# Top-2 gate dispatch on one core: transfers beside a change of direction are issued in smaller pieces

## The chip, the core and the metric

The kernel runs on one core of one Trainium2 chip. The metric is the device time of one execution in microseconds; where several runs are given, their median counts. The kernel before takes 242.45 us in the median of 9 runs (242.27 to 242.94).

## What is computed

For each of 16 x 1024 = 16384 tokens there are 8 router logits and a row of 512 fp32 values. The two largest softmax probabilities are scaled to sum to one, and the row is written out twice, once times each of the two weights.

```python
def reference(x, router_logits, k):          # x [16,1024,512], router_logits [16,1024,8], k = 2
    logits_max = np.max(router_logits, axis=-1, keepdims=True)
    probs = np.exp(router_logits - logits_max)
    probs = probs / np.sum(probs, axis=-1, keepdims=True)
    topk_indices = np.argsort(probs, axis=-1)[..., -k:]
    topk_probs = np.take_along_axis(probs, topk_indices, axis=-1)
    topk_probs = topk_probs / np.sum(topk_probs, axis=-1, keepdims=True)
    x_expanded = x[:, :, np.newaxis, :].repeat(k, axis=2)
    return (x_expanded * topk_probs[..., np.newaxis]).astype(np.float32)
```

In bytes: x is 33.55 MB, the logits are 0.52 MB, the output is 67.11 MB. Everything that is read is read once, and everything that is written is written once.

## The kernel before

The 16384 tokens are laid over 128 partitions, 128 tokens ("rows" below) on each, so that the rows of one partition lie one behind the other in memory. A row is 2 KB of input and 4 KB of output. A transfer of n rows therefore moves, for each partition, one unbroken stretch of n x 2 KB (a load) or n x 4 KB (a store).

First the logits come in with one transfer (L72). `top2_weights` finds the largest and second largest logit by a tree of max and min on VectorE, and ScalarE makes the two weights from their difference with two sigmoids (L41, L42). The weights of all rows stay in `WA`.

The rows are then worked through in two groups of 64 (`GROUP`). For each group:

- Four loads of 16 rows each (4.19 MB) go into `xs`, a buffer of 64 rows (L93 and L94).
- Six multiplications on VectorE (L97) follow `plan`: rows 0 to 15 into `osp`; rows 16 to 31 in place over `xs` rows 0 to 31; rows 32 to 39 and 40 to 47 into the two halves of `osp`; rows 48 to 55 and 56 to 63 over the two halves of `xs` rows 32 to 63. An output row is twice as long as an input row, which is why 16 rows fill 32 rows of `xs`.
- After each multiplication one store writes its rows (L103): 16, 16, 8, 8, 8, 8 rows, which is 8.39 MB for 16 rows and 4.19 MB for 8.

All transfers are issued by SyncE (SP) in the order of the program, and all go through its one queue. SP issues in order: an issue that has to wait holds up those behind it. What the issues wait for comes from the buffers: a store waits for its multiplication; the multiplication of rows 32 to 39 waits for the store that reads `osp`; the loads of the second group wait for the stores that still read their part of `xs`. The framework places these waits from the regions that each operation reads and writes.

Below, "load 1" to "load 4" and "store 1" to "store 6" are the transfers of a group in program order. Between the last load of a group and its first store, and between the last store of the first group and the first load of the second, the queue changes direction: load to store, store to load, load to store, three times in all.

Of the kernel before, what the change touches and what calls it, by code (L numbers as in the profile page):

```python
# [1 line left out]

# [4 lines left out]

F32 = mybir.dt.float32
ALU = mybir.AluOpType
ACTF = mybir.ActivationFunctionType  # L10
P = 128


def top2_weights(nc, pool, logits, M, E):

    hi, lo, n = None, None, E
    while n > 1:  # L20
        n //= 2
        if hi is None:
            a, b = logits[:, :, 0:n], logits[:, :, n : 2 * n]
            nhi = pool.tile([P, M, n], F32, tag=f"hi{n}")
            nlo = pool.tile([P, M, n], F32, tag=f"lo{n}")
            nc.vector.tensor_tensor(nhi, a, b, op=ALU.max)  # L26
            nc.vector.tensor_tensor(nlo, a, b, op=ALU.min)  # L27
        else:
            a, b = hi[:, :, 0:n], hi[:, :, n : 2 * n]
            nhi = pool.tile([P, M, n], F32, tag=f"hi{n}")  # L30
            nlo = pool.tile([P, M, n], F32, tag=f"lo{n}")
            tmp = pool.tile([P, M, n], F32, tag=f"tmp{n}")
            nc.vector.tensor_tensor(tmp, lo[:, :, 0:n], lo[:, :, n : 2 * n], op=ALU.max)  # L33
            nc.vector.tensor_tensor(nlo, a, b, op=ALU.min)  # L34
            nc.vector.tensor_tensor(nlo, nlo, tmp, op=ALU.max)  # L35
            nc.vector.tensor_tensor(nhi, a, b, op=ALU.max)  # L36
        hi, lo = nhi, nlo
    dlt = pool.tile([P, M], F32, tag="dlt")
    nc.vector.tensor_tensor(dlt, hi[:, :, 0], lo[:, :, 0], op=ALU.subtract)  # L39
    WA = pool.tile([P, M, 2], F32, tag="WA")  # L40
    nc.scalar.activation(WA[:, :, 0], dlt, ACTF.Sigmoid, scale=-1.0)  # L41
    nc.scalar.activation(WA[:, :, 1], dlt, ACTF.Sigmoid, scale=1.0)  # L42
    return WA


@with_exitstack
def kernel(
    ctx: ExitStack,
    tc: tile.TileContext,
    x: bass.AP,  # L50
    router_logits: bass.AP,
    k: bass.AP,
    out: bass.AP,
):
    nc = tc.nc
    B, S, D = x.shape
    E = router_logits.shape[-1]
    N = B * S
    assert int(k) == 2 and E == 8 and N % P == 0
    M = N // P  # L60

    GROUP = 64
    L = 16
    x_v = x.rearrange("b s d -> (b s) d").rearrange("(p m) d -> p m d", p=P)
    o_v = out.rearrange("b s k d -> (b s) k d").rearrange("(p m) k d -> p m k d", p=P)
    rl_v = router_logits.rearrange("b s e -> (b s) e").rearrange(
        "(p m) e -> p m e", p=P
    )

    wpool = ctx.enter_context(tc.tile_pool(name="wpool", bufs=1))  # L70
    logits = wpool.tile([P, M, E], F32)
    nc.sync.dma_start(logits, rl_v)  # L72
    WA = top2_weights(nc, wpool, logits, M, E)

    xs = wpool.tile([P, GROUP, D], F32)
    osp = wpool.tile([P, L, 2, D], F32)


    low = xs[:, : 2 * L, :].rearrange("p (r k) d -> p r k d", k=2)
    high = xs[:, 2 * L :, :].rearrange("p (r k) d -> p r k d", k=2)  # L80
    h = L // 2
    plan = [
        (0, L, osp),
        (L, L, low),
        (2 * L, h, osp[:, :h]),
        (2 * L + h, h, osp[:, h:]),
        (3 * L, h, high[:, :h]),
        (3 * L + h, h, high[:, h:]),
    ]

    for g in range(M // GROUP):
        m0 = g * GROUP
        for r in range(0, GROUP, L):  # L93
            nc.sync.dma_start(xs[:, r : r + L, :], x_v[:, m0 + r : m0 + r + L, :])  # L94
        for r, n, og in plan:
            rows = slice(m0 + r, m0 + r + n)
            nc.vector.tensor_tensor(  # L97
                og,
                xs[:, r : r + n, :].unsqueeze(2).to_broadcast([P, n, 2, D]),
                WA[:, rows, :].unsqueeze(3).to_broadcast([P, n, 2, D]),  # L100
                op=ALU.mult,
            )
            nc.sync.dma_start(o_v[:, rows], og)  # L103


# [1 line left out]
_INS = ['x', 'router_logits', 'k']  # L107
_OUTS = [((16, 1024, 2, 512), 'float32')]

_NUMBERS = {'k': 2}  # L110


# [26 lines left out]
```

## Time and profile before

| | |
|---|---|
| median of 9 runs | 242.45 us |
| the profiled execution's own time | 242.83 us |
| its span in the profile | 241.0 us |
| VectorE busy | 142.0 us (59% of the span) |
| ScalarE busy | 1.8 us |
| DMA packets' time, as a share of 16 engines' span | 98.4% |
| bytes moved, mean rate over the span | 101.19 MB, 420 GB/s |
| loads on L94 | 8, 4096 KB each |
| stores on L103 | 12: 8 of 4096 KB, 4 of 8192 KB |
| multiplication of 16 rows (128x16384) | 17.2 us |
| multiplication of 8 rows (128x8192) | 8.7 us |

The span is what the hardware profiler sees of one execution; 1.83 us of the execution's own time lie around it. A core has 16 DMA engines, and each transfer is cut into packets that are spread over them. The DMA share is the time in which these engines had a packet in hand. Times inside the profile count from the start of the span. The trace also keeps a record of each packet, with its start, its duration and its size.

### The profile page before, as it was taken

The numbers are of one execution on the slowest core, as the hardware profiler recorded it, in microseconds if no ns is written. First come the engines' busy times: TensorE is split into PE (matmuls) and PEld (weight loads), VectorE is DVE, ScalarE is ACT, GpSimd is POOL, SyncE is SP. The second block draws the span as 40 slices with busy tenths as digits, with TensorE's granted clock in tenths as the row PEclk, the third lists the DMA queues.
The fourth block names the chain that finished last, engine by engine and source line by source line (L and its number), as shares of the span: only waits on it lengthen the run. The fifth ranks groups of instructions, "written<-read, shape, count | busy, mean of one in ns | idle before, by whom it ended". The sixth has DMA issues, their size and how long they took to land.

```text
span 241.0 us, 112 instructions
## 1 busy us (share of the span) xinstructions
DVE 142.0 (59%) x23; ACT 1.8 (1%) x3; POOL 0.2 (0%) x4
## 2 busy tenths in 40 slices
DVE  2369999900399999400000999997007999990000
ACT  2000000000000000000000000000000000000000
POOL 0000000000000000000000000000000000000000
DMA  7999999998989899999999999999999999999994
GB/s 272 435 435 435 430 430 397 386 522 348 522 348 522 348 435 435 435 435 435 430 381 430 435 435 430 430 424 468 402 468 402 468 402 402 435 430 435 435 435 212
DMA packets 3024, 101.19 MB, mean 420 GB/s; under 512 B 336, under 2 KB 336, under 8 KB 464
## 3 DMA queue, kind: packets, MB, share of 16 engines
q1 hardware_dynamic: 3024, 101.19, 98.4%
HBM read 34.08 MB, written 67.11 MB: 420 GB/s over the span
## 4 chain that ended last, share of the span: by engine, by line
DMA 46%; DVE 36%; issue 7%; SPq 0%; DVEq 0%
DMA out_dram<-osp 27%; DVE osp L97 22%; DMA xs<-in_x_dram 19%; DVE xs L97 14%; SPq L72 0%; SPq L103 0%; DVEq L97 0%
## 5 line engine op out<-in xcount | busy, mean ns | idle before, releaser
L97 DVE TENSOR_TENSOR osp<-xs,WA 128x8192 f32<-128x8192 f32 (+1 forms) x6 | 69.0, 11534 | 70.2 <-DMA xs<-in_x_dram 40.0
L97 DVE TENSOR_TENSOR xs<-xs,WA 128x8192 f32<-128x8192 f32 (+1 forms) x6 | 69.2, 11536 | 0.2
L26 DVE TENSOR_TENSOR nhi<-logits 128x512 f32<-128x512 f32 x1 | 0.7, 692 | 4.4 <-DMA logits<-in_router_logits_dram 4.4
L41 ACT ACT_TABLE_LOAD x1 | 1.3, 1283 | 0.7 <-PEq L120 0.7
L33 DVE TENSOR_TENSOR tmp<-nlo 128x256 f32<-128x256 f32 (+1 forms) x2 | 0.7, 354 | 0.0
L36 DVE TENSOR_TENSOR nhi<-nhi 128x256 f32<-128x256 f32 (+1 forms) x2 | 0.7, 352 | 0.0
L35 DVE TENSOR_TENSOR nlo<-nlo,tmp 128x256 f32<-128x256 f32 (+1 forms) x2 | 0.7, 352 | 0.0
L34 DVE TENSOR_TENSOR nlo<-nhi 128x256 f32<-128x256 f32 (+1 forms) x2 | 0.7, 352 | 0.0
L27 DVE TENSOR_TENSOR nlo<-logits 128x512 f32<-128x512 f32 x1 | 0.7, 686 | 0.0
L41 ACT ACTIVATE WA<-dlt 128x128 f32<-128x128 f32 x1 | 0.3, 314 | 6.2 <-DVE dlt L39 6.2
L39 DVE TENSOR_TENSOR dlt<-nhi,nlo 128x128 f32<-128x128 f32 x1 | 0.3, 292 | 0.0
L42 ACT ACTIVATE WA<-dlt 128x128 f32<-128x128 f32 x1 | 0.3, 298 | 0.0
L120 POOL MEMSET const-bfloat16-1.0<- 128x1 bf16 x1 | 0.1, 103 | 0.0
L120 POOL MEMSET const-uint8-127<- 128x1 uint8 x1 | 0.1, 102 | 0.0
L120 POOL MEMSET const-float32-1.0<- 128x1 f32 x1 | 0.1, 100 | 0.0
L120 POOL MEMSET const-float32-0.0<- 128x1 f32 x1 | 0.1, 98 | 0.2 <-issue 0.2
## 6 DMA issues: line engine op xcount, KB each, us to landing
xs<-in_x_dram SPq DMA_DIRECT2D x8, 4096.0 KB, 36.6
out_dram<-osp SPq DMA_DIRECT2D x4, 4096.0 KB, 20.7
out_dram<-xs SPq DMA_DIRECT2D x4, 4096.0 KB, 22.7
logits<-in_router_logits_dram SPq DMA_DIRECT2D x1, 512.0 KB, 3.7
out_dram<-osp SPq DMA_DIRECT2D x2, 32.2
out_dram<-xs SPq DMA_DIRECT2D x2, 34.3
```

The costliest lines, as they stand in the source:

```text
L26: nc.vector.tensor_tensor(nhi, a, b, op=ALU.max)
L27: nc.vector.tensor_tensor(nlo, a, b, op=ALU.min)
L33: nc.vector.tensor_tensor(tmp, lo[:, :, 0:n], lo[:, :, n : 2 * n], op=ALU.max)
L34: nc.vector.tensor_tensor(nlo, a, b, op=ALU.min)
L35: nc.vector.tensor_tensor(nlo, nlo, tmp, op=ALU.max)
L36: nc.vector.tensor_tensor(nhi, a, b, op=ALU.max)
L39: nc.vector.tensor_tensor(dlt, hi[:, :, 0], lo[:, :, 0], op=ALU.subtract)
L41: nc.scalar.activation(WA[:, :, 0], dlt, ACTF.Sigmoid, scale=-1.0)
L42: nc.scalar.activation(WA[:, :, 1], dlt, ACTF.Sigmoid, scale=1.0)
L97: nc.vector.tensor_tensor(og, xs[:, r : r + n, :].unsqueeze(2).to_broadcast([P, n, 2, D]), WA[:, rows, :].unsqueeze(3).to_broadcast([P, n, ...
L120: nc = _bacc.Bacc("TRN2", target_bir_lowering=False, num_devices=1)
```

## The change

The loads of a group are cut into eight transfers of 4, 4, 8, 16, 16, 8, 4 and 4 rows, in place of four of 16. The first store of a group (16 rows) is issued as four transfers of 4 rows, and the last (8 rows) as two of 4 rows. The four stores between stay whole, and so do all six multiplications. The order of work on SP is otherwise the same.

```diff
+LOADS = [4, 4, 8, 16, 16, 8, 4, 4]
+STORE_ROWS = {0: 4, 56: 4}
...
     for g in range(M // GROUP):
         m0 = g * GROUP
-        for r in range(0, GROUP, L):
-            nc.sync.dma_start(xs[:, r : r + L, :], x_v[:, m0 + r : m0 + r + L, :])
+        r = 0
+        for n in LOADS:
+            nc.sync.dma_start(xs[:, r : r + n, :], x_v[:, m0 + r : m0 + r + n, :])
+            r += n
         for r, n, og in plan:
             rows = slice(m0 + r, m0 + r + n)
             nc.vector.tensor_tensor(
...
-            nc.sync.dma_start(o_v[:, rows], og)
+            for i in range(0, n, STORE_ROWS.get(r, n)):
+                t = STORE_ROWS.get(r, n)
+                nc.sync.dma_start(
+                    o_v[:, rows.start + i : rows.start + i + t], og[:, i : i + t]
+                )
```

In numbers: 21 transfers become 37 (1 for the logits, 16 loads, 20 stores). Beside a change of direction stand now loads of 4 rows (1.05 MB, 8 KB for a partition) and stores of 4 rows (2.10 MB, 16 KB for a partition), where loads of 16 rows (32 KB) and stores of 16 rows (64 KB) or 8 rows (32 KB) stood.

## The prediction

> **What bounds the kernel now.** I read the page first, for the engines and the DMA.
>
> ```profile
> DMA  7999999998989899999999999999999999999994
> GB/s 272 435 435 435 430 430 397 386 522 348 522 348 522 348 435 435 435 435 435 430 381 430 435 435 430 430 424 468 402 468 402 468 402 402 435 430 435 435 435 212
> q1 hardware_dynamic: 3024, 101.19, 98.4%
> ```
>
> The one queue keeps the 16 DMA engines busy for 98.4% of the span, and only the first and the last slice show real idle time. VectorE is busy 59%. So the time is that of the transfers, and the question is at what rate they run. (A packet's bytes count where it starts, so 522 and 348 in turn are one even rate seen through slices.) That the queue never runs dry is seen in the chain of waits and in SP's own waits:
>
> ```profile
> 1.16 12.96 DMA xs<-in_x_dram
> 31.48 32.56 DMA out_dram<-osp
> 99.28 33.51 DMA xs<-in_x_dram
> 150.13 31.88 DMA out_dram<-osp
> 208.16 8.69 DVE xs L97
> ```
> ```profile
> SPq L94 <- DMA out_dram<-xs: 21.6, 2, 11.5
> ```
>
> Columns of the first: start, duration, what. Store 1 of group 1 is issued at 31.48 and lands at 64.04, though 8.39 MB need only some 19 us: it stands behind loads 2 to 4. Load 1 of group 2, issued at 99.28, lands at 132.79 behind the stores. The last multiplication ends at 216.85, and the last store, issued at 216.88, lands 23.2 us later by the list of issues, at 240.08. In the second view SP waits 21.6 us for stores to leave `xs` before loads 3 and 4 of group 2 (issued at 112.40 and 122.89); when the later of them goes out, three loads (29 us of work) are still queued. No transfer starts late.
>
> These landings split the span into stretches that can be priced. From 182.01 to 240.08 there are only stores: store 2 (8.39 MB) and stores 3 to 6 (4.19 MB each), 25.17 MB in 58.07 us, 433.4 GB/s. That is the plain rate. The other stretches each hold one change of direction:
>
> - 14.12 to 64.04, loads 2 to 4 and store 1, 20.97 MB: 49.92 us, 48.39 at the plain rate, so 1.53 lost.
> - 64.04 to 132.79, stores 2 to 6 and load 1, 29.36 MB: 68.75 us against 67.75, so 1.00 lost.
> - 132.79 to 182.01, as the first: 49.22 us, so 0.83 lost.
>
> Together 3.36 us. The windows around the changes show where:
>
> ```profile
> 39.60:43.70 4.10, 4.10 (x1) 0.00 (x0) 0.00 (x0) 1.00 1.11 352
> 119.40:124.90 5.50, 0.00 (x0) 0.00 (x0) 0.00 (x0) 1.00 1.01 375
> 157.90:162.70 4.80, 4.80 (x1) 0.00 (x0) 0.00 (x0) 1.00 1.08 423
> 30.00:39.60 9.60, 9.57 (x2) 0.00 (x0) 0.00 (x0) 1.00 1.01 437
> ```
>
> The last two numbers of a row are DMA share and GB/s. The engines stay busy (share about 1) while the rate falls to 352 and 375 GB/s: packets take longer, nobody waits. The packet records say which. A 32 KB packet takes 1.21 us everywhere, but the last two of load 4 on each engine take 1.2 to 2.3 us in group 1 (up to 2.0 in group 2); at the store-to-load change the last store packet and the first two or three load packets take 1.3 to 1.9. By the mean over the engines this is 1.31, 0.76 and 0.51 us, 2.58 in all; the other 0.8 of the 3.36 is that the engines drift apart, from 0.6 to 1.8 us between first and last, and the last counts.
>
> **The change part by part.**
>
> *Sixteen more transfers on the DMA engines.* Each adds 8 packets and one completion per engine. The packet records price this: 4.19 MB in 32 KB packets stand 9.681 us apart from completion to completion on an engine, 8.39 MB in 64 KB packets 19.319. 2 x 9.681 - 19.319 = 0.043 us is the price of eight more packets and one more completion. 16 x 0.043 = +0.69 us, on the path, since the queue is never empty. From packet durations instead (queue lines of two windows: 1.214 us for 32 KB, 2.417 for 64 KB, so 0.011 for a packet, 0.09 for eight) it would be 16 x 0.09 = 1.4. I take 0.69, since durations overlap and completions don't, and keep 1.4 as the upper end. No packet of 8 or 16 KB is in the trace; the logits' 4 KB packets take 0.156 to 0.159 us once running, 26 GB/s on an engine where 32 KB packets make 27, so the middle sizes hold no surprise.
>
> *A rule that speaks against this.* In the stretch after 182.01 five stores run back to back at 433.4 GB/s, so a transfer's own latency does not show when the next one is queued. The Trainium skill ("DMA: Bandwidth & Descriptors", Rules for kernel authors, and Anatomy of one DMA) advises to merge small transfers, with 1 MiB as the size to reach, which the 4-row loads just do, and fits some 2 us of fixed cost to each transfer issued from GpSimd. By that figure alone 16 more would add 32 us and the time would be about 274 us.
>
> *Sixteen more issues on SP.* An issue takes 0.33 to 0.75 us, so 5 to 12 us more of SP time. Hidden: by queued work of 2.4 us per 1.05 MB piece at the start (four issues took 1.88), of 12 us at 31.48 (loads run on until 43.8), of over 20 us at 98.9. If the cover were gone, each issue would show in full.
>
> *Waits.* The first multiplication now needs three loads instead of one, two more completions, 0.09 us; its store is issued 12 us before the queue reaches it. Behind it on VectorE stand the other multiplications, which have the same 12 us. In group 2, loads 6 to 8 wait on SP for the two halves of store 6 (load 4 waited for the whole); behind them stand only later loads, with 29 us queued ahead. The multiplication of rows 32 to 39 may start up to 9.7 us earlier, when the first two pieces of store 1 have landed; stores 3 to 6 are then issued earlier into a full queue. Value: nothing.
>
> *The changes of direction.* The trace has no change with small packets, so I bound it. Lower end: what is slowed is a fixed time or a fixed number of bytes; nothing is saved. Upper end: all 3.36 us go. What the rows show is counted in packets: two at the load-to-store changes, one before and two or three after the store-to-load change. If that holds, the mean losses shrink with the packet: load to store (1.31 + 0.51) from 32 and 64 KB to 8 and 16 KB, to a quarter, saving 1.37; store to load (0.76) from 32 KB to 16 before and 8 after, to some 3/8, saving 0.47. Together 1.84. I leave the drift of the engines (0.8) where it is. Against it stands that two changes of the same sizes lost 1.53 and 0.83, so size isn't all.
>
> *Sum*, on the profiled execution: 242.83 + 0.69 - 1.84 = 241.68, that is 1.15 less. This execution lay 0.38 above the median, so against the median 242.45 - 1.15 = 241.3.
>
> **The rivals.**
>
> *A fixed loss (slower).* The engines read ahead of their writes by some number of bytes, and it is these bytes, not packets, that are slowed at a change. For it: 1.31 us at 27 GB/s is 35 KB, not a whole 64 KB store packet. Against: on every engine the slowing sits in the last two packets, whether engines turn together or 1.4 us apart. Place: the DMA engines' queue. Price: 16 x 0.043 = 0.69 with nothing saved, 243.1 us, up to 243.9 at 0.09 each. It decides as soon as the change saves less than 0.69 us of the 3.36.
>
> *The two cancel.* Only the small packets on one side of a change help, saving some 0.7 us: 242.4, no difference. The uneven losses at equal sizes speak for it.
>
> *All of it goes,* drift too: 242.45 + 0.69 - 3.36 = 239.8. Nothing says that the drift comes from size.
>
> *The change doesn't do what it says:* more transfers in flight choke issue, and the queue runs dry at a change. At 1 us for each of three changes plus 0.69 this gives about 246; the margins above speak against it.
>
> **How the numbers follow.** A measurement of this kernel can tell about 0.2%, 0.48 us, from no change. Smaller losses (241.3, own range 240.5 to 242.0, down to the 239.8 case at its edge): 0.48. Cancelling (242.4): 0.14. Fixed loss (243.1): 0.35. Choking: 0.03. Faster takes 0.46 of the first and 0.02 of the second: 0.48. Same takes 0.02, 0.10 and 0.05: 0.17. Slower: 0.02, 0.30 and 0.03: 0.35. The range goes from 240.5 to 243.4: below lies a tenth or less, above the dearest transfers and the choking.
>
> **What would show it.** Right: the rate around the three changes near 430 GB/s, long packets only of 8 and 16 KB, the stretch from the landing of store 1 of group 2 to the end longer by 0.04 us only (one transfer more, in store 6), DMA share still near 98%. Wrong: slow packets over as many bytes as before (64 KB on each engine), the three losses unchanged and the span up by 0.7; or issues on SP that wait for room, with gaps in the DMA row.

## The result, and the profile after

The changed kernel takes 241.65 us in the median of 9 runs (241.43 to 241.84). The kernel before takes 242.42 in 29 runs (242.12 to 242.99). The ratio is 0.9965, with a 95% interval of 0.9957 to 0.9974: faster by 0.35%; the two medians are 0.77 us apart. (A ratio here is taken from all runs of both kernels, so it is not exactly the quotient of the medians.) The profiled execution took 241.7 us, with a span of 239.9. The profiled execution of the kernel before (242.83) lay 0.41 above its median, so the two spans (241.0 and 239.9) differ by more than the two kernels do.

From the page of the changed kernel, the DMA's share by slices of 6 us, its rate, and the queue (packets, MB, share of 16 engines):

```profile
DMA  6999999999999899999999999999999998999996
GB/s 254 445 437 437 437 410 381 408 434 426 519 393 448 382 437 437 437 437 412 434 403 460 432 437 437 387 430 432 434 492 448 426 448 377 426 432 437 432 413 281
...
q1 hardware_dynamic: 5328, 101.19, 98.8%
```

The queue is as full as before, and the bytes are the same in more packets (5328 against 3024). The slice at 120 to 126 us, 381 GB/s before, is at 403 to 460 with its neighbours now: the store-to-load change costs little. The slices at 36 to 48 us still show 381 and 408 (397 and 386 before), where the plain rate is 437: the dip at the first change is still there.

The chain of waits of the same execution (start, duration, what) gives landings, and with them the stretches that the prediction priced:

```profile
2.09 12.10 DMA xs<-in_x_dram
...
32.92 31.09 DMA out_dram<-osp
...
93.44 38.71 DMA xs<-in_x_dram
...
150.92 29.95 DMA out_dram<-osp
```

Rows 0 to 15 of group 1 have landed at 14.19, store 1 at 64.01, rows 0 to 15 of group 2 at 132.15, store 1 of group 2 at 180.87. The stretches take 49.82, 68.14 and 48.72 us, against 49.92, 68.75 and 49.22 before, although they now hold 5, 3 and 5 transfers more at 0.043 us each. With that taken off, 0.31 us less is lost at the first change, 0.74 less at the second and 0.71 less at the third. These are landings, so the slowest engine counts and the drift of the engines is in them; the table below has means over the engines.

The windows around the three changes (the last two numbers of a row are DMA share and GB/s):

```profile
39.60:43.70 4.10, 4.10 (x1) 0.00 (x0) 0.00 (x0) 1.00 1.01 328
119.40:124.90 5.50, 0.00 (x0) 0.00 (x0) 0.00 (x0) 1.00 0.96 404
157.90:162.70 4.80, 4.80 (x1) 0.00 (x0) 0.00 (x0) 1.00 1.04 440
```

328 GB/s at the first change (352 before), 404 at the second (375), 440 at the third (423). The engines are busy in all three, so the slow packets of the first change are still there.

SP's own waits:

```profile
SPq L101 <- DMA out_dram<-xs: 19.1, 3, 9.6
SPq L101 <- DMA out_dram<-osp: 7.4, 1, 7.4
SPq L113 <- DMA xs<-in_x_dram: 3.8, 4, 1.8
```

The first row is the wait for `xs` that was there before (21.6 us then). The other two are new: a load that waits 7.4 us for a store out of `osp`, and stores that wait for loads. Nothing in the buffers asks for these; why they are there was not looked into. They cost nothing, since the queue stayed full. The multiplication of rows 32 to 39 starts at 54.36 instead of 64.13, after half of store 1, which brings nothing either.

### The profile page after: what moved, and what is told of

It is laid out like the page before. It is cut to its first block, busy times and chain, and to the rows that moved or that the text cites. A ratio compares the mean times of both kernels' runs of the same rounds, so it can differ in the third digit from the quotient of the medians.

```text
span 239.9 us, 137 instructions
## 1 busy us (share of the span) xinstructions
DVE 142.2 (59%) x23; ACT 1.8 (1%) x3; POOL 0.2 (0%) x4
## 2 busy tenths in 40 slices
DMA packets 5328, 101.19 MB, mean 422 GB/s; under 512 B 592, under 2 KB 592, under 8 KB 720
## 3 DMA queue, kind: packets, MB, share of 16 engines
q1 hardware_dynamic: 5328, 101.19, 98.8%
## 4 chain that ended last, share of the span: by engine, by line
DMA 47%; DVE 36%; SPq 3%; issue 0%; DVEq 0%
DMA out_dram<-osp 25%; DVE osp L105 22%; DMA xs<-in_x_dram 21%; DVE xs L105 15%; SPq L113 2%; SPq L101 1%; SPq L78 0%; DVEq L105 0%
```

## The experiments

All kernels have the loop of the changed kernel, with the sizes set for each group by itself:

```diff
-LOADS = [4, 4, 8, 16, 16, 8, 4, 4]
-STORE_ROWS = {0: 4, 56: 4}
+LOADS = [<group 1>, <group 2>]
+STORE_ROWS = [<group 1>, <group 2>]
...
-        for n in LOADS:
+        for n in LOADS[g]:
...
-            for i in range(0, n, STORE_ROWS.get(r, n)):
+            for i in range(0, n, STORE_ROWS[g].get(r, n)):
```

`C` stands for the cut loads of the change, [4, 4, 8, 16, 16, 8, 4, 4], and `W` for [16] * 4. Each kernel ran beside the kernel before on the same chip; the ratio is to that. The kernel before took 242.42 us beside the change, 242.55 beside before_again, loads_only, stores_only and middle_cut, 242.50 beside second_change, first_and_third, all_small and second_finer, and 242.51 beside the last four.

The table gives the time, and from the packet records of each kernel's one profiled execution what was lost at each change: the spacing of completions on an engine, over the last and the first 32 KB or more for each partition beside a change, above its price, as a mean over the 16 engines. The price, from the prediction's figures, is 1.205 us for each packet of 32 KB (an engine has eight packets of a transfer, one for each of 8 partitions; larger and smaller packets by their bytes) plus 0.043 us for each transfer. "Drift" is the time between the first and the last engine at the end.

| kernel | transfers | median us | ratio, 95% interval | 1st | 2nd | 3rd | drift |
|---|---|---|---|---|---|---|---|
| before | 21 | 242.42 | | 1.31 | 0.76 | 0.51 | 1.79 |
| before_again | 21 | 242.45 | 0.9997 (0.9984 to 1.0009) | 0.93 | 1.21 | 0.35 | 1.00 |
| the change | 37 | 241.65 | 0.9965 (0.9957 to 0.9974) | 1.12 | 0.11 | 0.10 | 1.05 |
| loads_only | 29 | 242.35 | 0.9987 (0.9977 to 0.9996) | 0.67 | 0.85 | 0.46 | 0.91 |
| stores_only | 29 | 242.36 | 0.9990 (0.9980 to 0.9999) | 1.19 | 0.55 | 0.49 | 1.92 |
| middle_cut | 37 | 242.48 | 0.9996 (0.9988 to 1.0005) | 0.68 | 1.31 | 0.09 | 0.81 |
| second_change | 24 | 241.14 | 0.9939 (0.9927 to 0.9952) | 1.33 | 0.19 | 0.04 | 0.87 |
| first_and_third | 31 | 242.62 | 1.0008 (0.9999 to 1.0016) | 1.26 | 1.21 | 0.34 | 1.02 |
| all_small | 65 | 242.76 | 1.0012 (1.0003 to 1.0021) | 0.17 | 0.53 | 0.14 | 1.17 |
| second_finer | 28 | 241.39 | 0.9950 (0.9937 to 0.9962) | 1.57 | 0.02 | 0.04 | 0.88 |
| g1_all_4 | 36 | 241.03 | 0.9939 (0.9926 to 0.9951) | 0.25 | 0.21 | 0.07 | 0.70 |
| g1_all_8 | 28 | 241.46 | 0.9950 (0.9938 to 0.9962) | 1.02 | 0.13 | 0.22 | 1.16 |
| g1_small_last | 30 | 241.22 | 0.9942 (0.9930 to 0.9954) | 0.81 | 0.14 | 0.09 | 0.82 |
| g1_small_first | 30 | 241.05 | 0.9944 (0.9930 to 0.9958) | 0.83 | 0.04 | 0.04 | 1.02 |

### The same kernel once more

```diff
+LOADS = [W, W]
+STORE_ROWS = [{}, {}]
```

> The loop of the changed kernel with the sizes of the kernel before (four loads of 16 rows, whole stores): the same 21 transfers. All theories: 242.4, ratio 1.000 within 0.0015. Its profile shows how far the three losses (1.31, 0.76 and 0.51 us by the mean of the engines) and the drift of the engines (0.6 to 1.8 us) vary from one execution to the next.

242.45 us, no difference. Its profile is worth more than its time. The first change lost 0.93 where it had lost 1.31, the second 1.21 for 0.76, and the drift was 1.00 for 1.79. The sum of the three is 2.49, and was 2.58. One change in one profile is known to some 0.4 us only; what is said below rests on differences larger than that, on several kernels that agree, or on times.

### Loads alone, stores alone

```diff
+LOADS = [C, C]
+STORE_ROWS = [{}, {}]
```

> Only the loads are cut (4, 4, 8, 16, 16, 8, 4, 4 rows), the stores stay whole: 8 transfers more, +0.34 us at 0.043 each. Size theory (what is lost at a change shrinks with the packets beside it, on whichever side they are small): load packets are small at all three changes, store packets at none; the second change keeps some 0.4 of its 0.76 us, the third goes from 0.51 to near 0.1, the first stays at 1.1 to 1.3 as with the full change; sum about 241.9. Read-ahead theory (each DMA engine reads ahead of its writes, every extra transfer anywhere uses up a little of that lead, and the lead is what is lost at a change from load to store): half as many extra transfers, half the effect, the third change keeps about 0.25, the second change is not told by it; about 242.1.

```diff
+LOADS = [W, W]
+STORE_ROWS = [{0: 4, 56: 4}, {0: 4, 56: 4}]
```

> Only the first and last store of a group are cut into pieces of 4 rows, the loads stay whole: 8 transfers more, +0.34 us. Size theory: the second change keeps the part behind it (0.40 of 0.76), the third keeps most of 0.51, because it is the last load packets that are slow there and they are 32 KB again; about 242.4. Read-ahead theory: as with the loads alone, about 242.1, the third change at about 0.25.

242.35 and 242.36 us, gains of 0.13% (0.04 to 0.23) and 0.10% (0.01 to 0.20). Together they give 0.23%, the full change 0.35%, a difference that lies within the intervals. The times are near the 242.4 that the size theory gave for stores_only, and above the 241.9 and 242.1 that the theories gave for loads_only. Each half helped its own side of the second change. Where the last stores were cut, the part before the turn was 0.10 (0.36 and 0.66 in the two profiles with the old sizes, 0.60 with only the loads cut). Where the first loads were cut, the part behind it was 0.25 (0.40 and 0.54 with the old sizes, 0.46 with only the stores cut), so the small loads alone took away about half of it, though their packets are a quarter as large. With both cut, as in the full change, the two parts are 0.02 and 0.09. The third change kept 0.46 and 0.49 in the two halves, where read-ahead by the number of transfers gave 0.25. In loads_only the load packets there are as small as in the full change, which lost 0.10: so small load packets alone don't cure it. Whether small packets on both of its sides would is told by first_and_third below.

### The same cuts at other places

```diff
+LOADS = [[16, 8, 4, 4, 4, 4, 8, 16]] * 2
+STORE_ROWS = [{16: 4, 40: 4}] * 2
```

> As many extra transfers as in the full change (16), but away from the changes of direction: loads of 16, 8, 4, 4, 4, 4, 8, 16 rows, the second store (16 rows) in four pieces and the fourth (8 rows) in two; beside each change stand the same sizes as before, save that the load at a change is the whole 16 rows and the stores are whole. Size theory: +0.69 us and nothing saved, 243.1, the three losses at 1.3, 0.76, 0.5. Read-ahead theory: the place doesn't matter, the third change loses nothing and the time is that of the full change, 241.6 to 241.8.

242.48 us, 0.9996: neither theory's number. As many cuts away from the changes bring nothing, so the place matters for the time. But they cost nothing either, though 16 transfers are 0.69 us: the first change (0.68) and the third (0.09) lost less in its profile, the second as much as ever (1.31).

### The second change alone, and all but it

```diff
+LOADS = [W, [4, 4, 8, 16, 16, 16]]
+STORE_ROWS = [{56: 4}, {}]
```

> Cut only beside the second change, store to load: the last store of group 1 in two pieces of 4 rows, the loads of group 2 in 4, 4, 8, 16, 16, 16 rows; all else whole. 3 transfers more, +0.13 us. Each-change theory (a change loses less when the packets on both of its sides are small, and only that change): the second change falls from the 0.8 to 1.3 us seen so far to about 0.1, the first keeps 0.9 to 1.3, the third 0.3 to 0.5; 242.4 - 0.9 + 0.1 = 241.6, as good as the full change with 3 transfers in place of 16. Read-ahead theory (every extra transfer anywhere eats some of the lead): 3 extra transfers do almost nothing, 242.3 or more.

241.14 us, ratio 0.9939 (0.9927 to 0.9952): better than the full change, with 3 extra transfers in place of 16, and better than the 241.6 of the each-change theory. The page and the chain of this kernel:

```profile
GB/s 274 433 433 438 438 438 378 411 504 372 482 394 438 394 438 438 438 433 397 430 413 468 433 427 422 433 482 438 438 427 449 383 493 361 427 438 438 438 438 263
...
q1 hardware_dynamic: 3456, 101.19, 98.7%
```
```profile
1.15 12.92 DMA xs<-in_x_dram
...
31.42 32.48 DMA out_dram<-osp
...
100.95 31.18 DMA xs<-in_x_dram
...
149.59 31.02 DMA out_dram<-osp
```

The dip at 36 to 48 us (378, 411) is still there. Store 1 of group 1 has landed at 63.90 and rows 0 to 15 of group 2 at 132.13: 68.23 us, where the prices make 67.86, so 0.37 is lost at the second change on the last engine (1.02 before, by the same prices). From the landing of rows 0 to 15 of group 2 (132.13) to that of its store 1 (180.61) it is 48.48 us, where the plain price is 3 x 9.681 + 19.319 = 48.36. So the third change lost 0.12 us on the last engine (0.86 before), with three whole loads of 32 KB packets ahead of it and a store of 64 KB packets behind: nothing was cut there. A part was paid ahead of it: each of the six loads of group 2 stands 0.03 to 0.04 us further from the one before it than its price, where loads 2 and 3 of the kernel before show 0.00.

The three losses in the table, less 0.13 us for the transfers, account for at most 0.8 to 0.9 of the 1.36 us between the medians. The table doesn't show the rest. How far the slowest engine ends behind the mean of the engines varies by as much (1.10 and 0.41 us in the two profiles with the old sizes, 0.45 here).

```diff
+LOADS = [[16, 16, 16, 8, 4, 4]] * 2
+STORE_ROWS = [{0: 4}] * 2
```

> The opposite: cut only beside the first and third change, load to store: loads of 16, 16, 16, 8, 4, 4 rows, the first store of a group in four pieces of 4 rows; all beside the second change whole. 10 transfers more, +0.43 us. Each-change theory: the second change keeps 0.8 to 1.3 us, the first about 1.0 (small packets did not cure it in the full change), the third 0.1 to 0.4; 242.4 to 242.8. Read-ahead theory: 10 of 16 extra transfers, so some 0.6 of the effect, about 241.9.

242.62 us, 1.0008 (0.9999 to 1.0016): no gain, at a price of 0.43 us for 10 transfers. The third change lost 0.34 with small packets on both of its sides, the first 1.26. Its chain:

```profile
90.56 42.39 DMA xs<-in_x_dram
...
151.56 30.38 DMA out_dram<-osp
```

132.95 to 181.94 is 48.99 us; 48.36 and five extra transfers make 48.58, so 0.41 lost, against 0.12 with whole transfers in second_change. Both kernels have six loads in group 2, so it isn't their number. By these two runs the small packets at the third change do little for it, and those at the second change nearly all; the other kernels with the second change cut on both sides (0.04 to 0.22 at the third) agree. One profile doesn't fit: middle_cut lost 0.09 at the third change after 1.31 at the second. It has eight loads in group 2, but so has loads_only with its 0.46, so this stays open.

### Everything small, and finer at the second change

```diff
+LOADS = [[4] * 16] * 2
+STORE_ROWS = [{0: 4, 16: 4, 32: 4, 40: 4, 48: 4, 56: 4}] * 2
```

> Every load and every store in pieces of 4 rows: 65 transfers, 44 more than before, +1.89 us. Each-change theory: the second change at 0.1, the third at 0.1, the first still about 1; 242.4 + 1.9 - 1.6 = 242.7 or a little less. Read-ahead theory: no lead is left at any change, the first included; all three near 0 and the drift under 1 us, 242.4 + 1.9 - 3.0 = 241.3. If an extra transfer costs 0.09 rather than 0.043 us, both come out 2 us higher.

242.76 us, 1.0012 (1.0003 to 1.0021). This is the number of the each-change theory, but not its reason: the first change, which no kernel so far had brought under 0.67, lost only 0.17. Its page:

```profile
DMA  7999999999999999999999999999999999999996
GB/s 259 422 425 422 425 418 429 425 429 429 434 434 434 434 434 434 432 434 434 426 376 423 423 419 425 419 434 432 432 432 434 432 432 429 429 433 426 432 432 258
```

No dip is left at 36 to 48 us (429, 425). But the plain rate of the loads is 418 to 425 instead of the 430 to 435 of the kernel before, so what was saved at the change is paid along the way. The second change lost 0.53 here, more than where only its own neighbours are small (0.02 to 0.21); one profile, and left open.

```diff
+LOADS = [W, [2, 2, 4, 8, 16, 16, 16]]
+STORE_ROWS = [{48: 4, 56: 2}, {}]
```

> As second_change, but finer: the fifth store in two pieces of 4 rows, the last in four of 2 rows (8 KB packets), the loads of group 2 in 2, 2, 4, 8, 16, 16, 16 rows. 7 transfers more, +0.30 us. Each-change theory: the second change is at its floor near 0.1 us already with 4 rows, so this only adds transfers: 0.1 to 0.2 us slower than second_change. If the loss goes on shrinking with the packets, the same or a little faster. Read-ahead theory: 7 extra transfers, some 0.3 us faster than second_change.

241.39 us. The second change lost 0.02, against 0.19 in second_change. Kernels with the same pieces of 4 rows there have lost from 0.04 to 0.21, so it isn't shown that the loss goes on shrinking with the packets. Four more transfers are priced at 0.17, and the time is no better: 4 rows are small enough.

### What sets the first change

Four kernels with the second change cut as in second_change, and the loads of group 1 in other sizes.

```diff
+LOADS = [<below>, [4, 4, 8, 16, 16, 16]]
+STORE_ROWS = [{56: 4}, {}]
...
+g1_all_4:       [4] * 16
+g1_all_8:       [8] * 8
+g1_small_last:  [16, 16] + [4] * 8
+g1_small_first: [4] * 8 + [16, 16]
```

> second_change (241.14 us) with the loads of group 1 in sixteen pieces of 4 rows: 12 transfers more, +0.52 us. Carried-lead theory (the engines' reads run ahead of their writes from the start of the loads; every small transfer eats about 0.03 us of that lead; what is left is lost when the loads end, 1.33 us in second_change): as in the run with all pieces small, the lead is gone after some transfers and the first change loses under 0.3; 241.1 + 0.5 + 0.3 - 1.1 = 240.8. Rival (in the run with all pieces small it was the small stores that spared the first change): it still loses 0.9 to 1.3; 241.5.

> second_change with the loads of group 1 in eight pieces of 8 rows: 4 transfers more, +0.17 us. Carried-lead theory: 4 times 0.03 more eaten, the first change still loses about 1.2; 241.2. Packet-bound theory (the lead can be no more than a number of packets, so it scales with the size of the load packets): half the loss, 0.65; 240.7.

> second_change with the loads of group 1 as 16, 16 and eight times 4 rows: 6 transfers more, +0.26 us. Carried-lead theory: the first change still loses about 1.1; 241.2 to 241.3. Packet-bound theory (the last packets before the change set the loss): as with all pieces of 4 rows, under 0.3; 240.4. If the packets at the start of the loads set the lead: 1.3, 241.4.

> second_change with the loads of group 1 as eight times 4 rows, 16, 16: 6 transfers more, +0.26 us. Carried-lead theory: 1.1 lost, 241.2 to 241.3, the same as with the small ones last. If the packets at the start set the lead: under 0.3, 240.4. If the last packets set it: 1.3, 241.4.

241.03, 241.46, 241.22 and 241.05 us: no clear step beyond second_change (241.14; by the ratios 0.9939 to 0.9950 against 0.9939), and the run with eight loads of 8 rows, if anything, a little slower. The first change lost 0.25, 1.02, 0.81 and 0.83. The last two are the telling pair: eight small loads at the end, next to the change, or at the beginning, far from it, make the same. So neither the packets beside the change nor those at the start set it; the readings by packet size at one end of the loads fall. What the loss goes with, over all fourteen profiles, is the number of loads in group 1: with 4 loads the first change lost 0.93 to 1.57 (mean 1.27 of five), with 6 loads 1.26, with 8 loads 0.67 to 1.12 (mean 0.87 of four), with 10 loads 0.82, with 16 loads 0.17 and 0.25. From 4 to 16 loads that is 1.06 us less for 12 loads, 0.09 for each. Single profiles overlap (0.93 with 4 loads, 1.12 with 8), as is to be expected when one is known to some 0.4 us. Every load is eight packets on each engine, so these kernels can't tell the number of loads from the number of packets or from their mean size.

A load more costs its 0.043 us, and in these kernels the spacing of the load completions shows another 0.03 for most loads after the sixth or so of group 1. So cutting the loads of group 1 pays about what it costs, as the times say.

This is what the theory of a carried lead says: the reads of an engine run ahead of its writes, each load uses up a little of the lead, and what is left is lost when the loads end. The counts fit its form, but not its size, which was put at 0.03 us for each load. That it is a lead of the reads is argued, not shown, since the packet records show only one start and one duration for each packet and not its two sides.

## Why the prediction was right, and where it was not

**The bound** held: the queue at 98.8% (98.4 to 99.2% in all fourteen profiles), no transfer late in any kernel, so the time is the transfers' own, plus what is lost at the changes.

**The price of a transfer** held: store pieces of 4 rows stand 4.862 us apart, which is half of 9.638 plus 0.043. The load pieces of 8 KB in group 2 stand 2.477 to 2.484 apart where 2.453 was expected; some 0.03 for each load was not foreseen, and all eight loads of group 2 pay it, the whole ones too (0.24 us in all, part of it counted at the second and third change). The Trainium skill ("DMA: Bandwidth & Descriptors", Anatomy of one DMA) has some 2 us of fixed cost for a transfer issued from GpSimd; here, on SP's full queue, 44 more transfers in all_small made the kernel 0.12% (0.03 to 0.21) slower, where 2 us each would be 88 us.

**Issues and waits** at nothing: held. The new waits of SP on other transfers were not foreseen; the full queue hid them.

**The changes of direction** are the step that was mis-sized, term by term. Forecast was that the loss shrinks with the packets at each change, 2.58 to 0.74 us by the mean. Measured is 2.58 to 1.33, 1.25 saved where 1.84 was forecast. Of its own signs of being right, a rate near 430 GB/s came at the third change (440), in part at the second (404), and not at the first (328).

- First change: 1.31 was to become 0.33; it is 1.12, and the unchanged sizes have shown 0.93. Here the rule by packet size is wrong, not only its factor. first_and_third, g1_small_last and g1_small_first show that packets beside the change don't set the loss; it goes with the number of loads ahead.
- Second change: 0.76 was to become 0.29; it is 0.11. Here the rule holds in direction on both sides of the turn, and with both cut it is stronger than proportional. Small packets on both sides lost 0.02 to 0.21 in seven kernels, whole ones 0.76 to 1.31 in four; all_small, with 0.53, stays unexplained.
- Third change: 0.51 was to become 0.13; it is 0.10, but for another reason, so the number was right by luck. With only the first and third changes cut it keeps 0.34; with only the second change cut it falls to 0.04.

**The drift** was left at its 0.8 us. It is lower in the profile after: by landings, drift included, the three changes lose 1.76 us less, by the mean of the engines 1.25, so some 0.5 of it went. The engines end 1.05 us apart where it was 1.79. But the kernel before has also been seen at 1.00, so this is mostly the execution that happened to be profiled.

**The sum** forecast 1.15 us less, 241.3; measured is 0.77 less. With 0.69 paid for the transfers, the saving is 1.46 us on the medians, against 1.84. The right case was named, and the missing part is mainly the first change.

**The rivals.** A fixed loss was the likeliest rival (chance 0.35), and it holds at one change of three, as far as the packets beside it go: at the first they save nothing that shows. (It isn't fixed in every way: with 16 loads ahead it was 0.17 and 0.25.) Its argument, that the first change's loss is not a packet's worth, was the better reading of that row. The prediction's argument for packets, that the last two packets were slow on every engine, was a coincidence of sizes: in the changed kernel the slow packets there are 8 KB, and 67 of the 128 of the last load take over a tenth longer than usual. They start from 3.4 to 0.3 us before the first engine turns; the 31 slow packets of 32 KB in the kernel before start from 3.7 to 0.8 us before it. Choking did not occur.

## What to carry to other kernels

When one full queue sets the time, price the change of direction by itself: take a stretch of one direction for the plain rate, and see what the stretches that hold a turn lose against it. Then cut only where a turn answers to it. Here it was the store-to-load turn, with the last store and the first 16 rows of loads cut into pieces of 1 to 2 MB; that gained 0.61% (0.48 to 0.73) with 3 extra transfers, where cutting at all turns gained 0.35% with 16. A loss that sits at one place may be made at another: the third turn was cured by cutting at the second. Why the packets slow down at a turn at all stays open.

## What the runs showed of the hardware that was not expected

- Packets slow down at a turn without the engines going idle: DMA share 1.01 at 328 GB/s in the changed kernel.
- The loss of a load-to-store turn depends on what came long before it: in the mean on the number of load transfers since the start (1.27 us with 4, 0.2 with 16), and on how the turn before was made (0.34 to 0.51 us at the third turn where the second was cut on one side or not at all, middle_cut apart; 0.04 to 0.22 where it was cut on both).
- Two executions with the same transfers shared out the loss over the first two turns differently (1.31 and 0.76, or 0.93 and 1.21), while the sum over all three was nearly the same (2.58 and 2.49 us).
